# A streaming-encoder block on one core: the first feed-forward by Strassen pairs, its down products dealt out between them, and the modulation sums moved to ScalarE and GpSimd

## The chip, the core and the metric

One core of a Trainium2 chip runs the whole program. The metric is the time of one execution on the device in microseconds (us); a run's time is that of the execution, and the profile is of one execution taken by itself. The core has five engines with a queue each: TensorE (PE; its weight loads are counted apart as PEld), VectorE (DVE), ScalarE (ACT), GpSimd (POOL) and SyncE (SP), which here only issues DMAs. An engine works through its queue in order.

## The reference

One layer on x of 512 tokens by 1024 features, in float32:

```python
mod = silu(c) @ w_ada + b_ada                    # nine vectors of 1024: shift, scale, gate, three times
h = rms(x) * (1 + s1) + sh1
x = x + 0.5 * g1 * ((silu(gate) * up) @ w_out)   # gate, up = halves of h @ ffn1_w_in; 1024 -> 2 x 2816 -> 1024
h = rms(x) * (1 + s2) + sh2
x = x + g2 * mixer(h)                            # gated delta rule (4 heads) and latent attention (4 heads)
h = rms(x) * (1 + s3) + sh3
x = x + 0.5 * g3 * swiglu(h, ffn2_w_in, ffn2_w_out)
```

## The kernel before, in words

Activations lie feature-major: eight tiles `xT[t]` of 128 features by 512 tokens. Each float32 product is made of three matmuls (`mm3`, L265): both factors are split into a high part (a ScalarE cast, `hh`, `wh`, `ah`) and a low part (VectorE, value minus high part: `hl`, `wl`, `al`), and high x high, high x low and low x high are added up in PSUM.

Weights come as *units* of 128x1024 (`unit`, L204): an SP load into `wr`, a ScalarE cast to `wh`, a VectorE subtraction to `wl`; each of the three has four buffers. With `dma=True` the low part is made by a ScalarE copy with scale -1 and an adding DMA from GpSimd's queue. Everything of 128x512 floats in SBUF shares one pool of 56 *slots* (L86). A DMA into a slot stands in SP's queue until the slot is free.

The stages: **phase 0** (L297) normalises x and runs over the eight feature tiles `kt`. In each turn it makes one tile of the first two modulation vectors (the matmuls of L418, a ScalarE copy `sg` L421, the matmuls of L338 that read `sg`, then VectorE), modulates `h[kt+1]` (`modulate`, L450: VectorE, ScalarE `hh`, VectorE `hl`) and adds the products of `h[kt]` into six accumulators: the first three feed-forward tiles f=0..2, gate and up. **First feed-forward**: for f=3..21 two dense units each, 24 matmuls of 512 columns per unit (L656), and `glu` (L618), which makes `ah` and `al`. **Down** (L678): eight output tiles t, each of 22 products over f; the last two in token halves, so that the norm of the first half (`norm_half`, L483) runs under the second. **Mixer** (L1965): `latents`, then 16 dense units (k, q, v, z) with the attention and delta-rule work in between, then the output product. **Second feed-forward** (L736 on): the last 18 f by *Strassen pairs*: token halves, input halves and gate/up form a 2x2x2 block product, which is done with seven products of 12 matmuls of 256 columns (`product`, L856) in place of the eight that the dense form amounts to. The weights are summed on VectorE before (`sums`, `sums2`, L785 and L790) and split (`u`, `x`, `y`, `g1`); the token sums t1..t4 are made by `token_sums` (L742); the partial results are taken out of PSUM by `early_copy` (L812) before the next product adds to them. Steps s are numbered by hand: pair j takes the steps 7j+0, 1, 3, 4, 6, 9 and 12 (`STEPS`, L30), a planner (`add`, `tick`) puts the splits and copies at their steps, and `down` (L902) deals the down products out among the steps.

The other seven **modulation vectors** (14 chunks of 512 columns): `ada_rest` (L549) loads 128x512 tiles of `w_ada`, eight to a chunk, and adds scale x tile into an accumulator on VectorE (L575, L577); `ada_columns` (L590) sums four accumulators over the partitions on PE (L596), copies them (L599), transposes (L603) and adds the bias. It runs as a side task: eight chunks under the first feed-forward, six under the down products. `mixer_consts` (L1083: rope tables, small vectors) is a second side task of the first feed-forward.

Order: inside `in_order` (L133) each engine gets its instructions in the order in which the Python code makes them; inside `behind` they only stay behind the end of such a block; elsewhere the scheduler of the language picks the order. Before the change phase 0 and the second feed-forward are `in_order`; the first feed-forward after phase 0 is not.

## Time and profile before

| | |
|---|---|
| median of 3 runs | 1047.33 us (1045.64 to 1049.43) |
| profiled execution: span | 1044.0 us |
| phase 0 | about 0 to 64 us |
| first feed-forward and down | 64 to 404 us |
| mixer | 404 to about 690 us |
| second feed-forward | 690 to 1044 us |
| PE busy 690 to 732 us (entry of the second feed-forward) | 41.8 of 42 us |
| ACT / DVE busy 700 to 732 us | 16.9 / 26.4 of 32 us |
| DMA share, 20 to 60 us / 60 to 80 us | 1.04 (280 GB/s) / 0.91 (269 GB/s) |

The span goes from the first to the last instruction of the profiled execution; the device time is a few us longer. Matmuls overlap in the pipeline, so their price is the distance between the starts of neighbours and not the duration that a row shows. In a row of the timeline the columns are start, duration, engine, line, operation, output <- inputs, shape, and count when several are merged; in brackets the idle time before and what ended it. In a row of one line's instructions the numbers are shortest/median/longest duration in ns.

### The profile page before, as it was taken

Reading aid. Unit: us, or ns where it says so; the run is one execution under the profiler, and the core shown is the slowest. Engines: PE = TensorE matmul, PEld = TensorE weight load, DVE = VectorE, ACT = ScalarE, POOL = GpSimd, SP = SyncE. Lnnn points to the kernel's source line nnn. Section 1 sums busy time; section 2 is a strip of 40 time slices with the busy share of each in tenths; the row PEclk is TensorE's granted clock in tenths of the full one; section 3 lists DMA queues with packets and bytes.
Section 4 is the critical chain, followed back from the end, with each engine's and each line's share of the span. In section 5 each row is a group of like instructions: output and inputs, shape, how many; then the busy total and the mean of one; then the engine's idle time right before and its main releaser. Section 6 shows DMA issues by size and latency. Waiting matters only on the chain. (4 is left out here: it accounts for less than half of the span.)

```text
span 1044.0 us, 16057 instructions
## 1 busy us (share of the span) xinstructions
PE 1026.9 (98%) x6355; PEld 881.4 (84%) x6355; DVE 681.4 (65%) x1257; ACT 446.9 (43%) x778; POOL 46.8 (4%) x113
## 2 busy tenths in 40 slices
PE   7999999999999999999999999999999999999998
PEld 5788878788887799888878778898999999999986
DVE  4488884333486636648977656688778778777633
ACT  4343222232222226749567563465445444344422
POOL 1000000000000011100001111310000000000000
PEclk9999999999999999999999999999999999999999
DMA  9989963323586539711311211073423334323222
GB/s 274 292 245 316 305 205 101 95 87 96 185 280 227 159 98 240 180 41 40 101 42 36 72 42 41 22 162 101 142 81 102 109 95 121 93 90 111 72 61 81
DMA packets 203689, 136.88 MB, mean 131 GB/s; under 512 B 13777, under 2 KB 186590, under 8 KB 203614
## 3 DMA queue, kind: packets, MB, share of 16 engines
q1 hardware_dynamic: 202318, 131.14, 42.8%
q0 software_dynamic: 1296, 4.72, 2.4%
q8 instruction: 50, 0.82, 0.3%
q14 instruction: 25, 0.20, 0.1%
HBM read 128.63 MB, written 2.49 MB: 126 GB/s over the span
## 5 line engine op out<-in xcount | busy, mean ns | idle before, releaser
L267 PE MATMUL pa<-hh,wh 128*128 128x512 f32 (+1 forms) x565 | 216.4, 383 | 0.4 <-ACT hh L465 0.4
L193 ACT CAST wh<-wr 128x1024 fp32r<-128x1024 f32 (+1 forms) x106 | 107.9, 1019 | 251.6 <-PE pa L268 172.9
L268 PE MATMUL pa<-hl,wh 128*128 128x512 f32 (+1 forms) x565 | 214.8, 380 | 0.5 <-DVE hl L457 0.3
L269 PE MATMUL pa<-hh,wl 128*128 128x512 f32 (+1 forms) x565 | 214.4, 379 | 0.0
L198 DVE TENSOR_TENSOR wl<-wr,wh 128x1024 fp32r<-128x1024 f32 (+1 forms) x97 | 114.2, 1179 | 95.6 <-ACT wh L193 93.1
L267 PE MATMUL pa<-ah,wh 128*128 128x512 f32 (+1 forms) x396 | 145.6, 368 | 0.6 <-DVE xT L899 0.4
L268 PE MATMUL pa<-al,wh 128*128 128x512 f32 (+1 forms) x396 | 144.5, 365 | 0.0
L269 PE MATMUL pa<-ah,wl 128*128 128x512 f32 (+1 forms) x396 | 143.5, 362 | 0.0
L267 PEld LDWEIGHTS pa<-hh,wh 128*128 128x128 f32 x565 | 106.3, 188 | 24.3 <-issue 3.7
L269 PEld LDWEIGHTS pa<-hh,wl 128*128 128x128 f32 x565 | 106.3, 188 | 21.0 <-issue 1.2
L268 PEld LDWEIGHTS pa<-hl,wh 128*128 128x128 f32 x565 | 106.4, 188 | 19.4 <-DVE hl L457 0.9
L269 PEld LDWEIGHTS pa<-ah,wl 128*128 128x128 f32 x396 | 74.8, 189 | 12.0
L267 PEld LDWEIGHTS pa<-ah,wh 128*128 128x128 f32 x396 | 75.2, 190 | 10.4 <-ACT wh L193 1.7
L268 PEld LDWEIGHTS pa<-al,wh 128*128 128x128 f32 x396 | 75.2, 190 | 7.2
L577 DVE SCALAR_TENSOR_TENSOR aa<-ar,sc,aa 128x512 f32<-128x512 f32 x98 | 73.0, 748 | 8.0 <-DMA ar<-in_w_ada 6.8
L872 PE MATMUL pb<-fh,wh 128*128 128x256 f32 x144 | 40.7, 283 | 0.0
L874 PE MATMUL pb<-fh,wl 128*128 128x256 f32 x144 | 40.7, 283 | 0.0
L874 PE MATMUL pb<-hh,wl 128*128 128x256 f32 x144 | 40.7, 283 | 0.0
L873 PE MATMUL pb<-fl,wh 128*128 128x256 f32 x144 | 40.7, 283 | 0.0
L873 PE MATMUL pb<-hl,wh 128*128 128x256 f32 x144 | 40.7, 282 | 0.0
L899 DVE SCALAR_TENSOR_TENSOR xT<-pa,mod,xT 128x512 f32<-128x512 f32 (+1 forms) x40 | 29.3, 735 | 17.3 <-PE pa L269 17.3
L872 PE MATMUL pb<-hh,wh 128*128 128x256 f32 x144 | 40.6, 282 | 0.0
(439 smaller groups left out, 1995.1 us busy)
## 6 DMA issues: line engine op xcount, KB each, us to landing
wr<-in_ffn_w_in SPq DMA_DIRECT2D x82, 512.0 KB, 3.9
ar<-in_w_ada SPq DMA_DIRECT2D x48, 512.0 KB, 6.0
wr<-in_ffn_w_out SPq DMA_DIRECT2D x34, 512.0 KB, 3.4
ar<-in_w_ada SPq DMA_DIRECT2D x48, 256.0 KB, 4.8
wr<-in_w_in SPq DMA_DIRECT2D x21, 512.0 KB, 3.7
wr<-in_ffn_w_out SPq DMA_DIRECT2D x17, 384.0 KB, 3.3
wl<-wr POOLq DMA_DIRECT2D x9, 512.0 KB, 6.2
wr<-in_w_out SPq DMA_DIRECT2D x8, 512.0 KB
```

The lines of the kernel that those rows point to most:

```text
L193: self.nc.scalar.copy(hi, raw)
L198: self.nc.vector.tensor_tensor(out=lo, in0=raw, in1=hi.bitcast(F32), op=ALU.subtract)
L267: mm(out, wh, xh, start=start, stop=False)
L268: mm(out, wh, xl, start=False, stop=False)
L269: mm(out, wl, xh, start=False, stop=stop)
L577: nc.vector.scalar_tensor_tensor(out=acc, in0=a, scalar=sc, in1=acc, op0=ALU.mult, op1=ALU.add)
L872: mm(out, wh, xh, start=start and k == 0, stop=False, **kw)
L873: mm(out, wh, xl, start=False, stop=False, **kw)
L874: mm(out, wl, xh, start=False, stop=stop and k == 3, **kw)
L899: nc.vector.scalar_tensor_tensor(out=self.xT[t][:, ts], in0=p[:, ts], scalar=gate[:, t:t + 1], in1=self.xT[t][:, ts], op0=ALU.mult, op1=AL ...
```

## The change

The first feed-forward now uses the same code as the second: f=0..2 come from phase 0, f=3 and 4 from four dense units (6..9), and f=5..21 are 17 Strassen pairs. The function `ffn2_rest` becomes `ffn_pairs`, with an entry (`enter1`, `enter2`) and an end (`leave1`, `leave2`) for each feed-forward. The token sums of the first feed-forward are made in phase 0, two calls a turn in the turns kt=3..6. The down products over f=0..15 are dealt out between the steps from s=9 on, those over f=16..21 stand at the end, tiles 4..7 in token halves. Everything from phase 0 to there is one `in_order` block. The modulation sums leave VectorE: ScalarE scales a tile (in place, but for the first of a chunk) and GpSimd adds it to the accumulator. Chunks 0..5 run in the entry (13 calls of two tiles) and in the first steps (two calls a step); chunks 6..13 and most of `mixer_consts` run as a fourth side task of the mixer's dense units.

```diff
@@ phase0
-        t, m = self.slot(s="hm"), self.slot(s="hm")
+        t, m = self.slot(s="hm"), self.tm[0]
...
-                    self.modulate([kt + 1], slice(0, NT), rb, self.c2, self.c1)
+                    self.modulate([kt + 1], slice(0, NT), rb, self.c2, self.c1, self.tm)
                     if kt == 0:
                         w = weights(kt + 1)
+                if j == 4 and kt >= KT // 2 - 1 and more:
+                    for which in range(2):
+                        drain(self.token_sums(kt + 1 - KT // 2, which))
+                if j == 1 and not more:
+                    tail()
@@ ada_rest becomes ada
+    def ada(self, chunks):
...
+        steps = [(c, kc) for c in chunks for kc in range(KT)]
...
+        for i in range(3):
+            load(i)
+        for i, (c, kc) in enumerate(steps):
+            a, sc = tiles.pop(i), self.sc[:, kc:kc + 1]
+            if kc == 0:
+                acc = self.slot(s="aa")
                 accs.append(acc)
+            out = acc if kc == 0 else a
+            nc.scalar.activation(out, a, AF.Copy, scale=sc)
+            if kc:
+                nc.gpsimd.tensor_tensor(out=acc, in0=acc, in1=a, op=ALU.add)
+            load(i + 3)
+            if i % 2:
+                yield
+        yield
+        yield from self.ada_columns(chunks[0], accs)
@@ ffn1
+        def tail():
+            for i in range(6, 10):
+                raws[i] = self.raw_unit(w1, i)
+            for i in (6, 7):
+                drain(self.unit_split(raws, split, i))
+        with self.in_order():
+            with self.tc.tile_pool(name="p0", bufs=3) as self.p0:
+                pu = self.phase0(tail)
+            accs = {i: pu[i // 2 + 3 * (i % 2)] for i in range(6)}
+            with self.tc.tile_pool(name="ws", bufs=1) as self.ws:
+                side, self.consts = Side(), self.mixer_consts()
+                side.add(self.ada((0, 1, 2, 3)), self.ada((4, 5)))
+                leave = self.ffn_pairs(w1, ins["ffn1_w_out"][0], lambda: self.mod[2], FIRST, raws, split, accs, self.enter1, side)
+        with self.tc.tile_pool(name="wx", bufs=2) as wx:
+            with self.behind():
+                nb = leave(wx)
@@ enter1 (products(i): one dense unit on PE; unit, of, glu: one half now, the VectorE half after the next entry's first half)
+        step = (side.step,)
+        side.step()
+        self.staggered([glu(0), step, (products, 6), unit(8), (do["load"],), glu(1), step, unit(9), (products, 7), step, glu(2),
+                        step, (do1["load"],), step, (products, 8), glu(3), step, of(do["sums"]), step, of(do["sums2"]), step,
+                        of(do["u"]), step, (products, 9), step, of(do["x"]), step, of(do["y"]), step, glu(4), of(do["g1"])])
@@ ffn_pairs
-        d0 = down(0, 4, 1, 1.3)
-        for c in (1, 2):
-            down(4 * c, 4, 28 * c + 10, 32 / 28)
-        down(12, 4, 94, 1.28)
+        if side:
+            d0, r = None, 128 / 103
+            for c in range(4):
+                down(4 * c, 4, stop - 103 + c * 32 / r, r)
...
             if s in last:
                 steps_of(*last[s])
+            if side:
+                side.step(2)
+                if s in (stop, stop + 8):
+                    next(self.consts)
...
+        def leave1(pool):
+            for t in (6, 7):
+                unit_hi(t, pool)
+                unit_lo(t)
+            halves = [slice(0, HALF), slice(HALF, NT)]
+            with self.matmuls_in_order(self.ends[mybir.EngineType.PE]):
+                for half, ts in enumerate(halves):
+                    for t in range(4, KT):
+                        for k in (0, 3):
+                            steps_of(t, k, k + 3, ts)
+                            if half and (t, k) in ((5, 0), (6, 3), (7, 3)):
+                                next(na, None)
+                        finish(t, ts, ends[t])
+                        self.square_in(t, ts, accum)
+                        if half and t in (4, 6):
+                            self.prefetch(t // 2 - 1)
+                    if half == 0:
+                        self.new_h()
+                        na = self.norm_half(0, accum, 3)
+                drain(na)
+                self.prefetch(3)
+            return self.norm_half(1, accum, 3)
@@ mixer
+        ada.add(self.consts, self.ada((6, 7)), self.ada((8, 9, 10, 11)), self.ada((12, 13)))
-        self.dense_units(4, Rates(sides, (1, 0, 0.25)), 1, conv_done(4, kT))
+        self.dense_units(4, Rates(sides, (1, 0, 0.25, 1)), 1, conv_done(4, kT))
-        self.dense_units(4, Rates(sides, (0.75, 0, 1.5)), 1, conv_done(0, qT))
+        self.dense_units(4, Rates(sides, (0.75, 0, 1.5, 1)), 1, conv_done(0, qT))
-        self.dense_units(4, Rates(sides, (0.75, 0.5, 1)), 1, conv_done(8, vT))
+        self.dense_units(4, Rates(sides, (0.75, 0.5, 1, 0.5)), 1, conv_done(8, vT))
-        self.dense_units(4, Rates(sides, (1, 0.75, 2)), 1, z_done)
+        self.dense_units(4, Rates(sides, (1, 0.75, 2, 0.5)), 1, z_done)
+        ada.flush()
```

More of the change, by code (lines that the diff above doesn't have):

```diff
@@ L333, in phase0 @@
         self.new_h()
+        self.new_sums(self.c1)
+        self.tm = [self.slot(s="tm") for _ in range(KT)]
         def columns(kt, sg, pg):
@@ L994, in ffn2_rest @@
-        for g in steps:
-            if isinstance(g, tuple):
-                g[0](*g[1:])
-                continue
-            next(g, None)
-            if waiting:
-                next(waiting, None)
-            waiting = g
-        next(waiting, None)
+        enter(raws, split, products, lambda f: self.glu_steps(accs, f), pairs, d0, side, w1)
         k0, m = 16, 6
@@ L1020, in steps_of @@
         def steps_of(t, a, b, ts=full):
-            if a == 0 and t not in ends:
-                ends[t] = self.aux() if t == 3 else self.acc()
+            if t not in ends:
+                ends[t] = self.aux() if t in ((3, 6, 7) if side else (3,)) else self.acc()
             self.dense(ends[t], units[t][1:], self.act[k0:], ts, a, b, m - 1)
@@ new lines, in leave2 @@
+        def leave2(pool):
+            for t in range(4, KT - 1):
+                steps_of(t, 0, m)
+                for e in range(2 * t - 8, min(2 * t - 6, t)):
+                    self.store(e, range(NB))
+                if t + 2 < KT:
+                    unit_hi(t + 2)
+                    unit_lo(t + 2)
+                finish(t, full, ends[t])
+            t = KT - 1
+            ends[t] = self.acc()
+            for half in range(2):
+                ts = slice(half * HALF, half * HALF + HALF)
+                steps_of(t, 0, m, ts)
+                finish(t, ts, ends[t])
+                if half == 0:
+                    self.store(t - 1, range(NB))
+                else:
+                    self.store(t, range(2))
+            self.store(t, range(2, 4))
@@ L1079, in bc @@
+        return leave1 if side else leave2
     def bc(self, col, n, w=P):
```

311 lines of the change are left out of this document (107 added, 204 removed).

## The prediction

> **What bounds the kernel now.** I read the page's head first, then the chain that ended last, then stretches.
>
> ```profile
> span 1044.0 us, 16057 instructions
> PE 1026.9 (98%) x6355; PEld 881.4 (84%) x6355; DVE 681.4 (65%) x1257; ACT 446.9 (43%) x778; POOL 46.8 (4%) x113
> ...
> PEclk9999999999999999999999999999999999999999
> ...
> PE 38%; DVE 1%; issue 1%; ACT 1%; POOL 0%; POOLq 0%; DVEq 0%
> ```
>
> PE is never without work for long, and at full clock; what the chain shows of other engines is 3%. The stretches view (length, then busy us and count of PE, PEld, DVE, ACT, POOL) says the same stage by stage:
>
> ```profile
> 64.10:404.00 339.90, 339.90 (x1652) 282.94 (x1650) 206.26 (x327) 101.55 (x132) 8.52 (x16) 1.00 0.60 182
> 440.00:600.00 160.00, 159.41 (x981) 128.31 (x979) 116.10 (x322) 100.83 (x208) 11.81 (x24) 1.00 0.22 57
> ```
>
> From 64 to 404 us, the stage that is rewritten, PE has no gap at all. So fewer matmuls are worth their full price, and any wait put into PE's queue costs its full length.
>
> **The matmuls: minus 13.5 us.** The price is the distance between starts (start, duration, engine, line, operands).
>
> ```profile
> 66.13 0.39 PE L267 MATMUL pa<-hh,wh 128*128 128x512 f32 x1
> 71.57 0.39 PE L267 MATMUL pa<-hh,wh 128*128 128x512 f32 x1
> 851.13 0.28 PE L872 MATMUL pb<-hh,yh 128*128 128x256 f32 x1
> 852.56 0.40 PE L267 MATMUL pa<-ah,wh 128*128 128x512 f32 x1
> 853.25 0.28 PE L872 MATMUL pb<-fh,wh 128*128 128x256 f32 x1
> L267 PE MATMUL pa<-ah,wh 128*128 128x512 f32 x132 | 51.7, 392 | 0.0
> L267 PE MATMUL pa<-ah,wh 128*128 128x256 f32 x88 | 25.3, 287 | 0.0
> ```
>
> A dense unit of 24 matmuls takes 71.57 - 66.13 = 5.44 us, 0.227 each. A Strassen product (12 of 256 columns) takes 852.56 - 851.13 = 1.43 us, 0.119 each, and three down matmuls between two products 0.69 to 0.70 us, 0.233 each. A pair's f costs 48 x 0.227 = 10.89 us dense and 84 x 0.119 = 10.0 by pairs; times 17, -15.2 us. Down was (the two rows of groups, times three) 396 x 0.227 + 264 x 0.119 = 121.2 us; it becomes 128 x 3 x 0.233 + 72 x 0.227 + 144 x 0.119 = 122.9, +1.7. Sum -13.5 us. The same code in the second feed-forward runs without gaps, so the steps from about s=9 on should too.
>
> **Phase 0: plus 9 us.** The token sums go into queues that are in order. One turn, and the prices of the sums from the second feed-forward:
>
> ```profile
> 47.61 0.75 DVE L457 SCALAR_TENSOR_TENSOR hl<-hm,sh,hh 128x512 fp32r<-128x512 f32 x1 [0.79 <-ACT hh L465]
> 48.40 1.09 PE L418 MATMUL pb<-ar,sc 128*32 128x256 f32 x16
> 49.58 0.37 ACT L421 COPY sg<-pb 128x256 f32<-128x256 f32 x1 [2.00 <-PE pb L418]
> 50.91 0.50 PE L338 MATMUL pb<-sel,sg 128*128 128x1 f32 x4
> 54.18 1.09 PE L418 MATMUL pb<-ar,sc 128*32 128x256 f32 x16
> L752 DVE TENSOR_TENSOR tv<-tm x4: 418/419/420, 700.2 to 707.9; 128x256 f32<-128x256 f32 x4
> L753 DVE SCALAR_TENSOR_TENSOR tv<-tm,mod,tv x4: 480/484/487, 700.9 to 708.3; 128x256 f32<-128x256 f32 x4
> L763 ACT CAST fh<-tv x8: 620/622/628, 701.5 to 725.5; 128x512 fp32r<-128x512 f32 x8
> L765 DVE TENSOR_TENSOR fl<-tv,fh x8: 682/685/693, 702.2 to 726.5; 128x512 fp32r<-128x512 f32 x8
> ```
>
> A turn is 54.18 - 48.40 = 5.78 us and VectorE ends it with `hl` at 48.36. Now two sums follow, each drained at once: 0.1 + 0.42 + 0.48 on VectorE, the cast 0.62, `fl` 0.69, 2 x 0.48, the second cast 0.62, less the overlap of neighbours: 3.8 us until ScalarE is free. Behind that cast stands `sg` of the next turn: 52.1 to 52.5, not 49.58. PE's L338 is due at 50.91 and waits 1.5 us. That turn's split, `hh` and `hl` are late as well, so the later turns start the sums 0.8 us after PE's turn begins and each L338 waits 2.4 us. Sums after kt=3, 4, 5 delay the L338 of three turns: 1.5 + 2.4 + 2.4. After kt=6 no L338 is left, but `hl` of the last tile is 0.65 us late, and the first dense unit's low part, behind two sums, one cast (0.95) and one subtraction (1.22), comes 6.85 us into the last turn where PE asks at about 4.9: 2.0. Sum 8.9, I take 9. Below it: 0, if the order in the block were not what the code says; above: 12, if DMA, 0.9 to 1.0 busy here, is late too.
>
> **The entry: plus 28 us.** The prices:
>
> ```profile
> 439.89 2.56 ACT L1308 ACTIVATE uh<-ur,cwT 128x512 fp32r<-128x512 f32 x4
> 59.04 1.99 ACT L193 CAST wh<-wr 128x1024 fp32r<-128x1024 f32 x2
> L621 ACT ACTIVATE sg<-pa x22: 584/587/592, 60.9 to 270.4; 128x512 f32<-128x512 f32 x22
> L623 DVE TENSOR_TENSOR af<-sg,pa x19: 676/687/690, 75.5 to 275.3; 128x512 f32<-128x512 f32 x19
> L626 DVE TENSOR_TENSOR al<-af,ah x22: 680/684/693, 65.7 to 277.3; 128x512 fp32r<-128x512 f32 x22
> L198 DVE TENSOR_TENSOR wl<-wr,wh x97: 951/1224/1227, 25.7 to 657.3; 128x1024 fp32r<-128x1024 f32 x81, 128x768 fp32r<-128x768 f32 x16
> L1232 POOL TENSOR_TENSOR Sg<-S,gl x2: 1040/1040/1041, 631.6 to 643.1; 128x512 f32<-128x512 f32 x2
> 377.43 1.23 DVE L198 TENSOR_TENSOR wl<-wr,wh 128x1024 fp32r<-128x1024 f32 x1 [0.52 <-ACT wh L193]
> 377.80 1.45 POOL L481 TENSOR_TENSOR na<-na,sq 128x256 f32<-128x256 f32 x1 [101.46 <-ACT sq L479]
> 665.10 0.74 POOL L481 TENSOR_TENSOR na<-na,sq 128x256 f32<-128x256 f32 x1
> ar<-in_w_ada SPq DMA_DIRECT2D x48, 256.0 KB, 4.8
> ```
>
> I count from the start of phase 0's last turn. *PE*: the unit held above ends at 12.1, three more at 28.4, and two products with a short wait for `u`'s low part at 31.8. There, in step s=2, stands `ada_columns` of chunks 0..3: 13 calls in the entry and two a step make the 18th call, the one that issues it, fall in s=2. Being in order, PE can do nothing else until the 32nd tile is added up.
>
> *ScalarE* starts on the side task at 6.45. Until the 32nd tile it has 32 scalings x 0.615 (four of the same form in 2.46 us between starts) = 19.7; five glus, in each of which it waits for VectorE between `sg` and `ah`, x 1.85 = 9.3; six casts of 128x1024 x 0.95 = 5.7; 0.8 more. It is through at 42.0, and GpSimd at 43.1: PE waits 11.3 us. The columns then cost 0.8 more than before, as transposes stand right behind their copy. The second group (chunks 4, 5) stands in s=7. ScalarE must first take a partial result out of PSUM after s=3 (47.8), then 12 scalings, one cast of each size: 57.0, GpSimd 58; PE is there at 52.1: 5.9. Together 18 us from ScalarE alone. SP's queue adds no reserve: 48 of these tiles (last row: 256 KB each) and the first pairs' weights are some 16 MB in 60 us, about 270 GB/s; and a tile's load that waits for a slot, which only GpSimd's add sets free, holds the pairs' weight loads behind it.
>
> *GpSimd* makes it longer. A 128x512 operation took it 1.04 us, and the 128x256 add of 665.10 took 0.74, but 1.45 when it began under VectorE's `wl<-wr,wh`: that ended at 378.66, 0.86 us into the add. Two operands in SBUF on VectorE seem to hold GpSimd up. If they exclude each other, the first group ends no earlier than 7.7 + 28 adds x 1.04 + VectorE's two-operand work (five `al`, five low parts of 1.22, one of 0.69, six sums of 0.68: 14.3) = 51.1, and PE waits 19.3; the second 14 x 1.04 + 7.1 later, 72.8, where PE is at 60.0: 12.8. Together 32 us. With adds at 0.74 the port is no bound and 18 stays; with 1.46, twice the 128x256, it is 50. I take 28: near the port's sum with the one row of the full width, as some of VectorE's work falls into time when GpSimd has nothing to add.
>
> The Trainium skill ("SBUF — State Buffer", section "SBUF: two separate sides") speaks against this change here: GpSimd and a VectorE instruction with two SBUF inputs take one port pair by an exclusive lock, held for a whole instruction. The trace agrees at 377.80, where 0.74 became 1.45. Its "GPSIMD Engine Reference", section 3.1, gives 4497 ns for a GpSimd add of 2048 columns; a quarter of it, 1.12 us, is an estimate from that page, and with it the port's sum would be 3 us longer.
>
> **The end of down: plus 5 us.** The second half of tiles 4..7 (24 x 0.357 = 8.6 us) must cover the first half's norm, where 44 x 0.357 = 15.7 us did.
>
> ```profile
> 384.35 0.48 DVE L685 SCALAR_TENSOR_TENSOR xT<-pa,mod,xT 128x256 f32<-128x256 f32 x1 [5.69 <-PE pa L269]
> 390.35 0.59 PE L445 MATMUL pb<-dg,ones 128*128 128x256 f32 x2
> 400.85 0.28 PE L267 MATMUL pa<-hh,wh 128*128 128x256 f32 x1
> 402.73 0.49 DVE L457 SCALAR_TENSOR_TENSOR hl<-hm,mod,hh 128x256 fp32r<-128x256 f32 x1 [0.18 <-ACT hh L465]
> ```
>
> Now the last `hl` of that half comes 18.9 us after the first half's last `finish`, just as PE reaches it. After, PE reaches it at about 9.6 + 2.5 = 12; the norm can be there at 14.5 at best (spread at 7.5, then eight tiles of 0.8 on VectorE), at 18.9 if nothing gets faster. 2 to 7, I take 5: the splits for the mixer's first units stand in the same stretch.
>
> **The mixer: plus 4 us.** 64 scalings x 0.615 = 39 us are added to ScalarE's 100.8 of 160 us (the row above), 56 adds to GpSimd's 11.8, the rope tables to VectorE's 116. All still fit, PE's 159.4 of 160 has no slack, and waits there are scheduled, not forced: 0 to 10. Less than 0 is excluded, as PE has no gap there, nor in down, that work taken from VectorE could close.
>
> **Sum.** -13.5 + 9 + 28 + 5 + 4 = +32.5 us on the profiled execution, whose span is 1044.0; the median of the runs is 1047.33, 3.3 us of it outside the span, which nothing here changes. 1047.3 + 32.5 = **1080 us**. The case's own range takes the entry from 24 to 50, the end from 2 to 7, the mixer from 0 to 10: +21.5 to +62.5, 1069 to 1110.
>
> **The rivals.**
> *Order by readiness (faster).* If the engines' queues in the block did not bind as the code reads, with `sg` and the casts issued ahead of the sums and scalings, phase 0 and the entry would cost nothing. It decides at `sg`: it must start within 1.3 us of L418's end in turns 4 to 6. Then -13.5 + 2 to 9: 1036 to 1043, say 1037. For it: the second feed-forward's entry, with the same eight token sums, ran without a gap. Against: that entry has five units on PE over it and no scalings.
> *The entry fits, phase 0 doesn't.* If the adds and scalings reach PE's two places in time, but for 5 us, the sum is -13.5 + 9 + 5 + 2 to 5 = about +3, 1050; no change. It needs 0.30 us a scaling in place of 0.615.
> *No shared port.* 18 in the entry: +22, 1070.
> *The pairs save nothing.* They would have to cost 0.130 us a matmul; the row says 0.119, so it gets no chance of its own.
>
> **How the numbers follow.** Forecast 0.5, of it 0.05 beyond 1100; no shared port 0.2; entry fits 0.1; order by readiness 0.2. A run of three can tell 0.3%, 3.1 us, from no change. Faster by more than that: 0.2; within: 0.09; slower: 0.71. Leaving out the fastest part of the one rival and what lies above 1100, the range is 1038 to 1100.
>
> **What would show it.** Steps: a dense unit and a product at the same 5.44 and 1.43 us; in phase 0 an idle PE before L338, three times, ended by `sg`; in the entry PE idle before the `ada_columns` matmuls, twice, ended by GpSimd's adds, over 10 us the first time; GpSimd's adds longer than 1.04 us where VectorE subtracts; a gap before the mixer's first products ended by `hl`. It is wrong if PE stays at 98%, or if the adds take under 0.8 us.

## The result, and the profile after

The changed kernel takes 1157.73 us (1156.54 to 1162.03, four runs) against 1046.92 us (1045.64 to 1049.43, four runs) of the kernel before on the same chip: 1.106 times as long, with a 95% interval of 1.104 to 1.109. The forecast was 1080 us, from 1038 to 1100. The sign was right, and the size was out by more than the whole growth that was forecast: 111 us came where 33 were expected.

The head of the page of the changed kernel, and the shares of its chain that ended last:

```profile
span 1154.8 us, 17725 instructions
...
PE 1054.9 (91%) x6911; PEld 916.5 (79%) x6911; DVE 770.9 (67%) x1362; ACT 562.9 (49%) x999; POOL 189.0 (16%) x213
...
PEclk9997679999999998999999969999999999999999
...
PE 71%; DVE 10%; ACT 7%; POOL 5%; issue 4%; DMA 2%; SPq 0%; POOLq 0%; ACTq 0%; DVEq 0%
```

PE has fallen from 98% to 91%. The chain now leaves PE for VectorE, ScalarE, GpSimd, the issue of instructions and DMA, for 28% of the span; before, they had some 3%, in a chain whose shares add up to only 41%. And PE's granted clock falls in three places, most in the fourth to sixth of the 40 slices (87 to 173 us) and in the 24th (664 to 693).

The first and the last start of the dense half units that stand at the mixer's and at the second feed-forward's head cut the span into three (the view of one source line: durations min/median/max, first and last start). First the kernel before, then the changed one:

```profile
L510 PE MATMUL pa<-hh,wh x32: 280/283/468, 404.1 to 695.6; 128*128 128x256 f32 x32
```

```profile
L522 PE MATMUL pa<-hh,wh x32: 278/283/561, 460.0 to 806.4; 128*128 128x256 f32 x32
```

To the mixer 404.1 became 460.0 (+55.9). The mixer, 291.5, became 346.4 (+54.9). What follows took 1044.0 - 695.6 = 348.4 and takes 1154.8 - 806.4 = 348.4. So half of the loss lies where the forecast looked for all but 4 us of it, and half in a stage that it had down for 4.

**The entry.** The start of phase 0's last turn and PE's longer waits behind it in the changed kernel's timeline (start, duration, instruction, and in brackets the idle time before it with what ended it), then GpSimd's adds, and then the stretches view (length; PE, PEld, DVE, ACT, POOL busy and count; clock; DMA share; GB/s):

```profile
68.09 0.39 PE L271 MATMUL pa<-hh,wh 128*128 128x512 f32 x1
...
101.23 0.58 PE L865 MATMUL pb<-hh,wl 128*128 128x256 f32 x1 [4.96 <-DVE wl L800]
111.85 1.91 PE L599 MATMUL pb<-aa,ones 128*32 128x512 f32 x2 [4.83 <-POOL aa L586]
122.55 1.92 PE L599 MATMUL pb<-aa,ones 128*32 128x512 f32 x2 [8.79 <-POOL aa L586]
135.82 0.58 PE L863 MATMUL pb<-fh,yh 128*128 128x256 f32 x1 [5.16 <-ACT uc L807]
145.43 1.92 PE L599 MATMUL pb<-aa,ones 128*32 128x512 f32 x2 [4.77 <-POOL aa L586]
155.69 1.92 PE L599 MATMUL pb<-aa,ones 128*32 128x512 f32 x2 [8.35 <-POOL aa L586]
```

```profile
80.88 41.61 POOL L586 TENSOR_TENSOR aa<-aa,ar 128x512 f32<-128x512 f32 x25 [1.37 <-ACT ar L584]
134.17 21.47 POOL L586 TENSOR_TENSOR aa<-aa,ar 128x512 f32<-128x512 f32 x14 [11.67 <-ACT ar L584]
```

```profile
100.00:120.00 20.00, 7.70 (x28) 4.92 (x28) 13.66 (x10) 10.18 (x16) 19.14 (x13) 0.59 0.37 114
120.00:140.00 20.00, 11.51 (x50) 9.57 (x51) 4.54 (x6) 7.24 (x11) 8.02 (x6) 0.59 0.48 171
140.00:160.00 20.00, 6.88 (x21) 3.28 (x20) 7.09 (x6) 7.69 (x14) 14.93 (x11) 0.58 0.38 118
160.00:180.00 20.00, 20.00 (x140) 18.47 (x139) 15.28 (x23) 8.08 (x12) 0.00 (x0) 0.99 0.27 79
```

The mechanism of the forecast is there to the letter: PE stands in front of `ada_columns` (L599), twice for each group, until GpSimd's adds end. The first group ends at 122.5, 54.4 us after phase 0's last turn began at 68.1 (the first row above, of which the turn has six), where 51.1 were worked out. But ahead of those waits (at 101.23) and between them (at 135.82) there are others, of 5 us each, for a split that VectorE and a copy that ScalarE made late. PE is busy 26 of the 60 us from 100 to 160, at a clock of 0.59. From 160 on PE runs without a gap.

**The mixer.** The whole stage in the stretches view, before and after, and the longest wait of the changed kernel's PE in it (timeline):

```profile
404.00:695.50 291.50, 286.30 (x2069) 240.49 (x2069) 199.40 (x516) 172.64 (x360) 35.21 (x56) 1.00 0.31 81
```

```profile
460.00:806.00 346.00, 309.45 (x2094) 250.95 (x2095) 236.73 (x579) 211.61 (x423) 110.33 (x143) 0.94 0.37 106
```

```profile
673.83 1.08 PE L1952 MATMUL pb<-ident,on 128*128 128x128 f32 x4 [8.05 <-DVE on L1228]
```

PE's idle time grew from 5 to 37 us, and its busy time by 23 us at a lower clock. No other engine is near its limit over the stage: VectorE has 237 of 346 us, ScalarE 212, GpSimd 110. No single wait is longer than the 8 us shown. The profile alone doesn't say which part of the moved work this is; the experiments below take it apart.

### The profile page after: what moved, and what is told of

Its sections match the earlier page's. It is cut to its first block, busy times and chain, and to the rows that moved or that the text cites. A ratio compares the mean times of both kernels' runs of the same rounds, so it can differ in the third digit from the quotient of the medians.

```text
span 1154.8 us, 17725 instructions
## 1 busy us (share of the span) xinstructions
PE 1054.9 (91%) x6911; PEld 916.5 (79%) x6911; DVE 770.9 (67%) x1362; ACT 562.9 (49%) x999; POOL 189.0 (16%) x213
## 4 chain that ended last, share of the span: by engine, by line
PE 71%; DVE 10%; ACT 7%; POOL 5%; issue 4%; DMA 2%; SPq 0%; POOLq 0%; ACTq 0%; DVEq 0%
PE pa L271 11%; PE pa L272 10%; PE pa L273 10%; PE pb L863 10%; PE pb L864 9%; PE pb L865 9%; POOL aa L586 5%; DMA ar<-in_w_ada 2%; ACT ar L584 1%; DVE wl L207 1%; DVE cv L1434 1%; PE pb L273 1%; PE pb L271 1%; PE pb L272 1%; ACT hh L477 1%
## 5 line engine op out<-in xcount | busy, mean ns | idle before, releaser
L586 POOL TENSOR_TENSOR aa<-aa,ar 128x512 f32<-128x512 f32 x98 | 139.6, 1426 | 185.5 <-ACT ar L584 141.7
L271 PE MATMUL pa<-hh,wh 128*128 128x512 f32 (+1 forms) x277 | 105.4, 380 | 5.4 <-ACT hh L477 2.1
L272 PE MATMUL pa<-hl,wh 128*128 128x512 f32 (+1 forms) x277 | 103.9, 375 | 1.4 <-DVE hl L469 0.9
L273 PE MATMUL pa<-hh,wl 128*128 128x512 f32 (+1 forms) x277 | 103.4, 373 | 0.5 <-DVE wl L207 0.5
L865 PE MATMUL pb<-hh,wl 128*128 128x256 f32 x280 | 80.8, 289 | 5.0 <-DVE wl L800 5.0
L863 PE MATMUL pb<-hh,wh 128*128 128x256 f32 x280 | 80.8, 289 | 0.8 <-ACT wh L795 0.8
L864 PE MATMUL pb<-hl,wh 128*128 128x256 f32 x280 | 80.6, 288 | 0.0
L584 ACT ACTIVATE ar<-ar,sc 128x512 f32<-128x512 f32 x98 | 66.7, 719 | 11.4 <-DMA ar<-in_w_ada 10.0
L271 PEld LDWEIGHTS pa<-hh,wh 128*128 128x128 f32 x277 | 53.1, 192 | 19.0 <-issue 4.2
L273 PEld LDWEIGHTS pa<-hh,wl 128*128 128x128 f32 x277 | 52.9, 191 | 10.9 <-DVE wl L207 1.4
```

The source lines that it names most:

```text
L271: mm(out, wh, xh, start=start, stop=False)
L272: mm(out, wh, xl, start=False, stop=False)
L273: mm(out, wl, xh, start=False, stop=stop)
L584: nc.scalar.activation(out, a, AF.Copy, scale=sc)
L586: nc.gpsimd.tensor_tensor(out=acc, in0=acc, in1=a, op=ALU.add)
L863: mm(out, wh, xh, start=start and k == 0, stop=False, **kw)
```

## The experiments

Each run is one execution, with its profile. Two readings are used throughout: the start of the mixer ("to mixer") and its length, taken from the same source line as above. What follows the mixer is within 1 us of 348.4 in every run that is read below by its stages. For scale: single runs of the kernel before, made beside them, took 1046.03 to 1049.17.

| run | to mixer | mixer | time, us |
|---|---|---|---|
| before | 404.1 | 291.5 | 1046.92 |
| changed | 460.0 | 346.4 | 1157.73 |
| no_adds | 432.6 | 332.6 | 1114.96 |
| mixer_no_adds | 459.7 | 332.5 | 1141.97 |
| vector_sums | 442.9 | 339.7 | 1132.37 |
| mixer_vector_sums | 459.3 | 339.3 | 1148.40 |
| mixer_loads_only | 459.5 | 318.8 | 1128.11 |
| mixer_no_rope | 461.3 | 322.1 | 1133.13 |
| mixer_no_sums | 459.2 | 294.6 | 1103.60 |
| mixer_neither | 460.9 | 295.5 | 1106.11 |
| no_entry_mixer_columns | 407.1 | 302.7 | 1059.85 |
| entry_loads_mixer_loads | 425.7 | 311.1 | 1086.82 |
| order_in_phase0 | 455.8 | 348.0 | 1153.75 |
| before_scalar_gpsimd | 416.4 | 291.8 | 1058.28 |
| no_sums | 405.0 | 293.9 | 1048.65 |
| no_sums_sums_order | 404.6 | 314.0 | 1068.38 |
| sums_no_columns_held | 405.0 | 342.1 | 1096.89 |
| mixer_loads_held | 404.9 | 311.6 | 1066.29 |
| mixer_loads_own | 404.8 | 307.4 | 1061.98 |
| after_own | 462.5 | 344.7 | 1157.01 |

### GpSimd's adds

Everywhere (no_adds), or in the mixer alone (mixer_no_adds, with `c > 5`):

```diff
-            if kc:
-                nc.gpsimd.tensor_tensor(out=acc, in0=acc, in1=a, op=ALU.add)
```

> The changed kernel without GpSimd's 98 adds of the modulation sums (each acc keeps only its first row block's product, so the seven other row blocks are left out of the sums); ScalarE's scalings, the loads and the columns stay where they are, and the static order of the tensor engine moves in about one row of a hundred. Theory A, the adds delay the columns and hold VectorE's port: the mixer loses 40 to 55 of its 55 us of growth and the entry 20 to 34 of its 52, so 1068 to 1098 us. Rival B, ScalarE's scalings and the loads set the columns: within 10 of the changed kernel's 1158. Rival C, the entry is the adds' but the mixer's 55 us come from something else that moved (the rope tables, the order): the entry loses 20 to 34 and the mixer nothing, 1124 to 1138.

> As the run without adds, but only for chunks 6 to 13, those summed in the mixer; the entry keeps its adds. Theory A: the mixer, 346 us from its first matmul to the first of the second feed-forward, falls to 291 to 306, the time to 1103 to 1118. Rivals B and C: the mixer stays within 8 us of 346 and the time at 1150 to 1160. The stretch ahead of the mixer stays at 460 by all of them.

The entry loses 27.4 us, as theories A and C had it; the mixer loses 13.9, which is neither A's 40 to 55 nor C's nothing. The total, 1115, falls between their ranges. So leaving out the adds takes away half of the entry's loss and a quarter of the mixer's. The two stages don't disturb each other: the mixer is 332.6 and 332.5 us with a different entry. That allowed later runs to make one edit in each stage.

How the adds act on VectorE is seen at a very small instruction of the mixer (one source line; min/median/max ns). First the changed kernel, then the run without adds:

```profile
L1930 DVE SCALAR_TENSOR_TENSOR va<-al x8: 160/164/1267, 613.2 to 709.9; 128x2 f32<-128x2 f32 x8
```

```profile
L1928 DVE SCALAR_TENSOR_TENSOR va<-al x8: 141/161/165, 577.4 to 668.3; 128x2 f32<-128x2 f32 x8
```

Two columns a partition take 0.16 us, but beside the adds as much as 1.27, about the length of one add. In the changed kernel's timeline three of the eight are long (1.06, 1.27 and 1.09 us, from 613.23, 617.04 and 645.64), and these three lie within runs of adds; the five of 0.16 lie outside them. The forecast had GpSimd stand behind VectorE; it also goes the other way. That is the exclusive lock, held for a whole instruction, of the Trainium skill's "SBUF — State Buffer", section "SBUF: two separate sides", and the row agrees with it in size.

### The sums on VectorE, in the places of the change

vector_sums, and for the mixer alone mixer_vector_sums:

```diff
-            nc.scalar.activation(out, a, AF.Copy, scale=sc)
-            if kc:
-                nc.gpsimd.tensor_tensor(out=acc, in0=acc, in1=a, op=ALU.add)
+            if kc:
+                nc.vector.scalar_tensor_tensor(out=acc, in0=a, scalar=sc, in1=acc, op0=ALU.mult, op1=ALU.add)
+            else:
+                nc.vector.tensor_scalar(out=acc, in0=a, scalar1=sc, scalar2=None, op0=ALU.mult)
```

> The changed kernel with all 112 steps of the modulation sums as one VectorE instruction each, in the same places, nothing of them on ScalarE or GpSimd; the result is the reference's. Theory A: VectorE's 0.75 us a step lie where it has room in the entry only in part; the entry loses 15 to 30 us and the mixer 30 to 50, 1080 to 1110. Rival B (ScalarE's queue and the loads): if the queue, the same as A; if the loads, the entry loses less than 8. Rival C: mixer stays, 1125 to 1143.

> The same for chunks 6 to 13 alone. Theory A: the mixer falls by 30 to 50 of its 55 us, 1108 to 1128. Rival C: within 8 of 1158. If VectorE is itself the mixer's bound (it is at 20.00 of 20 us busy in one stretch of the changed kernel), the time rises by up to 64 times 0.75 = 48 us.

With 1132.37 us the first lands in C's range; the second gains 7.1 us in the mixer, less than A asked and more than C. One VectorE instruction a step, which the kernel before used, is 25 us better here than the pair of ScalarE and GpSimd, though VectorE is the busier engine. But 85 us of the 111 stay: the larger part isn't the choice of engine.

### The mixer taken apart

Four kernels without the mixer's sums in some part. mixer_loads_only reads the last loaded tile of each chunk as if it were the sum; mixer_no_sums replaces the three `ada` generators by constants; mixer_no_rope leaves out the mixer's adds and sets the rope tables to a constant, mixer_neither leaves out sums and tables. The edit of mixer_no_sums:

```diff
-        ada.add(self.consts, self.ada((6, 7)), self.ada((8, 9, 10, 11)), self.ada((12, 13)))
+        ada.add(self.consts)
+        for j in (5, 6, 7, 8):
+            self.mod[j] = self.const([P, 8], s="mod")
+            nc.gpsimd.memset(self.mod[j], 0.1)
```

> Chunks 6 to 13 are loaded, and each column is made from the last row block's tile as it was loaded: the 64 scalings on ScalarE and the 56 adds on GpSimd are left out, loads and columns stay. The run without the mixer's adds had a mixer of 332.5 us, 41 above the 291.5 of the kernel before. Theory S, ScalarE's 64 scalings (45 us in its queue, 172 us to 217) push the casts and copies of attention back: the mixer falls by 25 to 41 us, to 291 to 307 and the time to 1100 to 1117. Theory R, the rope tables and norm columns that now come at the mixer's start are what is late: it stays within 5 us of 332 and the time at 1137 to 1147. Theory D, the loads of the sums hold up the weights and the copies through DRAM: the same, no gain.

> As the run without the mixer's adds, and the rope tables (positions, angles, sines, cosines, some 70 small VectorE instructions, 14 us) are constants set by GpSimd instead of computed in the mixer. Theory R: the mixer falls by 20 us or more, to 312 or less, the time to 1122 or less. Theory S: at most 8 us of 332, the time 1134 to 1142. Theory D: nothing.

> Chunks 6 to 13 are left out altogether (loads, scalings, adds, columns; their vectors are constants), the rope tables stay in the mixer. Theory S: 5 us (the columns) to 8 below the run with loads alone. Theory D: 25 to 41 us below the run without the mixer's adds, while the run with loads alone gains nothing. Theory R: within 10 of 1142.

> Neither the sums of chunks 6 to 13 nor the rope tables are computed (constants in their place): the mixer holds then less than that of the kernel before, which computed no sums but had the tables ready too. If sums and tables are the whole of it, the mixer is 288 to 294 us and the time 1098 to 1104. Rival O, the static order or what the mixer finds when it starts (weights not yet there, a late ScalarE) costs of itself: the mixer stays 10 us or more above 291.5.

Without the scalings the mixer falls by a further 13.7 us, about half of the least that theory S asked for. Without loads and columns it falls by 24.2 more, where S had 5 to 8, to 294.6, and is then 3.1 us above the kernel before. The rope tables cost nothing when no sums are there (294.6 and 295.5) and 10.4 beside loads and scalings (332.5 and 322.1): not a cost of their own, then, but one that comes up only beside the sums. So theory R falls in the form that it had (10.4 lies between its 20 and S's 8), S explains a quarter, and with the sums out neither what the mixer finds at its start nor the order that it then has costs more than 4 us (rival O asked for 10).

### Loads against columns, and the entry

One edit in each stage:

```diff
# no_entry_mixer_columns: no sums in the entry; in the mixer columns of constant tiles
+                    if i == 0:
+                        accs.append(self.slot(s="aa"))
+                        nc.gpsimd.memset(accs[-1], 0.1)
# entry_loads_mixer_loads: loads alone; columns only for c < 6
-            nc.scalar.activation(out, a, AF.Copy, scale=sc)
-            if kc:
-                nc.gpsimd.tensor_tensor(out=acc, in0=acc, in1=a, op=ALU.add)
+            if kc == 7:
+                accs[-1] = a
...
-        yield from self.ada_columns(chunks[0], accs)
+        if chunks[0] < 6:
+            yield from self.ada_columns(chunks[0], accs)
```

> Two edits in two stages. Chunks 0 to 5 are left out (no loads, scalings, adds or columns; their vectors are constants), and in the mixer the columns of chunks 6 to 13 are made from tiles that GpSimd sets to a constant: no loads, scalings or adds there. Start to mixer: if the sums are the whole of the entry's growth, 404 - 13.5 (matmuls) + 9 (token sums of phase 0) + 7 (end of the down products) = 406, between 402 and 412; if another part of the change costs there, above 420. Mixer (294.6 without sums, 318.8 with loads and columns): theory D, the 64 loads take slots and the queue, 297 to 303; theory C, the tensor engine stands in order behind the columns, 310 to 319. Time 1053 to 1063 by D, 1066 to 1080 by C.

> Two edits in two stages. Chunks 0 to 5: loads and columns stay, the columns are made from the last row block's tile as loaded (no scalings, no adds). Chunks 6 to 13: the 64 loads stay, nothing reads them and there are no columns; the vectors are constants. Start to mixer (460 with all, 432.6 without adds): if the 48 loads at 300 to 390 GB/s hold the entry, 420 to 432; if ScalarE's scalings do, 408 to 416. Mixer: theory D 310 to 319, theory C 295 to 302.

In the mixer both count: columns 302.7 - 294.6 = 8.1, loads 311.1 - 294.6 = 16.5, and 24.6 together is what mixer_loads_only had shown (24.2). Both mixers lie in theory D's ranges, at the upper and the lower end: the loads are two thirds, but C's columns are the last third. The columns are PE's own work rather than a wait: in the first of these mixers PE is busy 296.5 us and idle 6.2, in no_sums 288.0 and 5.9.

Without the entry's sums the mixer starts at 407.1 here, and at 405.0 in a later run (no_sums): inside the 402 to 412 expected. Loads and columns bring it to 425.7, inside the range given for loads that hold the entry. In entry_loads_mixer_loads a row of PE's waits there (us in all, times, longest) and two stretches say how:

```profile
PE pb L597 <- DMA ar<-in_w_ada: 10.8, 3, 4.4
```

```profile
64.00:100.00 36.00, 34.13 (x156) 27.25 (x154) 25.01 (x38) 16.10 (x24) 0.00 (x0) 0.96 0.91 302
100.00:120.00 20.00, 11.85 (x56) 8.21 (x56) 8.01 (x11) 5.44 (x9) 0.00 (x0) 0.70 0.80 278
```

The transfers run at 302 GB/s with the DMA engines 91% busy, and PE waits for them 10.8 us in front of the columns, which read one tile of each chunk as it was loaded; nothing is scaled or added. Then the scalings add 6.9 us (425.7 to 432.6) and the adds 27.4.

### Two orders, and one part of the change alone

order_in_phase0 puts the token sums behind the next turn's column products and weight casts, and four squares behind two casts at the end of the down products:

```diff
-                if j == 4 and kt >= KT // 2 - 1 and more:
-                    for which in range(2):
-                        drain(self.token_sums(kt + 1 - KT // 2, which))
+                if j == 0 and kt >= KT // 2:
+                    drain(*(self.token_sums(kt - KT // 2, which) for which in range(2)))
```

> The changed kernel with two reorderings, the whole of the reference computed: each pair of token sums in phase 0 comes behind the next row's column products and weight casts, its two halves interleaved, and the squares of the first four outputs at the end of the down products come behind the casts of the last two weight units. By the forecast's working the waits of phase 0's column sums (1.5 + 2.4 + 2.4 us, and up to 2.6 of its tail) and the 2.4 us behind the squares go: start to mixer 460 to between 450 and 454, the time 1147 to 1152. Rival: the token sums only wait elsewhere, 0 to 3 us, 1155 to 1158.

It gains 4.2 us ahead of the mixer, less than the 6 to 10 forecast and more than the rival's 0 to 3. The waits of the changed kernel's column sums, which are the forecast's to a few tenths (1.5, 2.4, 2.4),

```profile
46.78 0.60 PE L344 MATMUL pb<-sel,sg 128*128 128x1 f32 x4 [1.30 <-ACT sg L433]
54.99 0.61 PE L344 MATMUL pb<-sel,sg 128*128 128x1 f32 x4 [2.13 <-ACT sg L433]
63.20 0.61 PE L344 MATMUL pb<-sel,sg 128*128 128x1 f32 x4 [2.15 <-ACT sg L433]
```

are gone, 5.6 us, and so are the 2.4 behind the squares. In their place PE waits for `hh` of the next tile, 2.9 us in the rows below, and for its `hl`, 0.9, which leaves the 4.2:

```profile
50.84 0.50 PE L271 MATMUL pa<-hh,wh 128*128 128x512 f32 x1 [1.19 <-ACT hh L476]
57.59 0.50 PE L271 MATMUL pa<-hh,wh 128*128 128x512 f32 x1 [0.35 <-ACT hh L476]
64.35 0.49 PE L271 MATMUL pa<-hh,wh 128*128 128x512 f32 x1 [1.38 <-ACT hh L476]
```

before_scalar_gpsimd is the kernel before with its sums as ScalarE scalings and GpSimd adds:

```diff
-                        if kc + e == 0:
-                            nc.vector.tensor_scalar(out=acc, in0=a, scalar1=sc, scalar2=None, op0=ALU.mult)
-                        else:
-                            nc.vector.scalar_tensor_tensor(out=acc, in0=a, scalar=sc, in1=acc, op0=ALU.mult, op1=ALU.add)
+                        nc.scalar.activation(a if kc + e else acc, a, AF.Copy, scale=sc)
+                        if kc + e:
+                            nc.gpsimd.tensor_tensor(out=acc, in0=acc, in1=a, op=ALU.add)
```

> The kernel before with one part of the change alone: its modulation sums, where they are, as 112 scalings on ScalarE and 98 adds on GpSimd in place of 112 VectorE instructions. They lie spread over the first feed-forward and the down products there. Theory of place (the cost lies in where the sums come, not in the engines): within 8 us of 1047. Rival, the adds cost wherever they are (27 us in the entry and 14 in the mixer of the changed kernel): 1062 to 1090.

1058.28 against 1046.20 of the kernel before beside it: 12 us, between the two ranges. All of it lies ahead of the mixer (416.4), and nearly all in one stretch, the first of these two (length, then busy us):

```profile
120.00:160.00 40.00, 32.97 (x131) 25.82 (x132) 25.67 (x34) 21.30 (x31) 24.74 (x17) 0.87 0.76 226
280.00:320.00 40.00, 40.00 (x178) 33.16 (x177) 18.01 (x16) 22.89 (x32) 25.40 (x25) 1.00 0.72 236
```

Both stretches have some 25 us of GpSimd, and the second costs nothing. PE's two longest waits ahead of the mixer from 60 us on, 3.8 us each, are both for VectorE (`af` and `rw`). Spread out, the pair of engines is cheaper than in the entry but not free; that place decides the rest is what the two stretches suggest, not what a run shows.

### No sums at all; the order, the work, the places

Two parts of the mixer's loss, loads and scalings, are waited for by hardly any instruction of PE. But with them the planner puts PE's instructions in another order: 749 of the 1613 that the program has there stand elsewhere, dense units earlier and attention later. Three kernels hold PE to a given order (edit below, with a list of places): one without sums to the order with them, two with sums to the order without. They stand against one without any sums:

```diff
-    nb = k.mixer(nb)
+    with k.traced() as block:
+        nb = k.mixer(nb)
+    held = [i for i in block if i.engine == mybir.EngineType.PE]
+    for a, b in zip(PE_ORDER, PE_ORDER[1:]):
+        k.follow(held[b], held[a].name)
```

> The changed kernel with no modulation sums at all (all 14 chunks left out, their vectors constants): the pairs and the moved tables alone. From the stages measured: 407 to the mixer, 295 in it, 348 behind it and 2 around the span, 1050 to 1054. If the stages do not add up, outside that.

> No sums at all, but the tensor engine's instructions of the mixer are held in the order that they have when the mixer's sums are there (loads, scalings and adds, without columns); 749 of the 1613 stand elsewhere by that. Theory O (the order carries the cost of loads and scalings): the mixer takes 310 to 330 us and the time 1066 to 1086. Theory W (the work itself carries it): the mixer stays at 293 to 299 us, the time 1050 to 1056.

> No sums in the entry; in the mixer the loads, scalings and adds of chunks 6 to 13 without their columns (vectors constants), with the tensor engine's instructions of the mixer held in the order of the kernel without sums. In its own order this mixer would take 346 - 8 = 338 us. Theory O: with the order held only the adds' 14 us are left, 302 to 314 us, 1058 to 1072. Theory W: 330 to 345 us, 1086 to 1102.

> No sums in the entry; in the mixer the 64 loads alone, nothing reads them, with the tensor engine's instructions held in the order of the kernel without sums. In its own order this mixer took 311.1 us. Theory O: 294 to 299 us, the time 1050 to 1056. Theory W (slots and queue): 308 to 314 us, 1064 to 1070.

no_sums came 1.4 us under its range, at 1048.65. The order without the work costs 20 us (314.0), as theory O had it. The work without the order costs as much as with it: 311.6 against 311.1 for the loads, and 342.1 against some 338 (an estimate, 346 less the columns' 8) for all but the columns, as theory W had it. Each is enough by itself and they don't add up. So the other order isn't needed to make the work dear; the work costs as much in either order.

Last, the loads into three tiles of their own, by themselves and in the full changed kernel:

```diff
-                tiles[i] = self.slot(s="ar")
+                tiles[i] = self.ad.tile([P, NT], F32, tag="ar", name=self.name("ar"))
...
-        self.late_enter(12)
+        self.late_enter(9)
```

> No sums in the entry; in the mixer the 64 loads alone, nothing reads them, no columns, as in the run whose mixer took 311.1 us, but into three tiles of their own and not into the pool of 56 that the mixer's other tiles come from (the pool for late tiles has 9 places for that, not 12). Queue, number and bytes are the same. Theory P (places in the shared pool): the mixer is back at 293 to 299 us, the time 1048 to 1054. Theory Q (the queue, or the bytes): it stays at 308 to 314 us, 1063 to 1069.

> The changed kernel whole, with the mixer's 64 loaded tiles in three places of their own; the accumulators stay in the shared pool. Start to mixer stays at 460. Theory P: the loads' 16.5 us go in large part, the mixer 328 to 336 us and the time 1139 to 1148. Theory Q: within 3 us of 346 and 1158.

307.4 us lies between the ranges, 0.6 below Q's, and the full kernel, with 1.7 gained in the mixer and 0.7 in all, lies in Q's: theory P falls as the main cause. Where a large part of the loads' cost now lies is seen in mixer_loads_own (waits of ScalarE and PE in the mixer, then a stretch at its start):

```profile
ACT wh L202 <- DMA wr<-in_w_in: 14.8, 1, 14.8
...
PE pa L271 <- ACT uh L1306: 5.9, 1, 5.9
```

```profile
427.00:447.00 20.00, 14.01 (x64) 11.06 (x63) 5.42 (x9) 4.67 (x8) 1.04 (x1) 0.88 0.88 257
```

As nothing reads these tiles, they are all fetched in the first 90 us of the mixer (issued up to 492.1), and there ScalarE waits 14.8 us for a weight that stands behind 17 of them in SP's queue. That shows one way in which the loads cost time, the queue or the bytes that they share with the weights. That it is the same in the changed kernel, where the loads are spread over 180 us, isn't shown: another queue for them wasn't tried. By what mechanism the loads cost 16.5 us there stays open.

## Why the prediction was wrong, step by step

Every step of the sum beside what the runs give for it:

| step | forecast | measured | from |
|---|---|---|---|
| matmuls, phase 0, end of down | -13.5 + 9 + 5 = +0.5 | +0.9 | no_sums 405.0, before 404.1 |
| entry | +28 (24 to 50) | +55.0 | changed 460.0, no_sums 405.0 |
| mixer | +4 (0 to 10) | +54.9 | 346.4 and 291.5 |
| second feed-forward | 0 | 0.0 | 348.4 and 348.4 |

**The first line came out right in part by luck.** Phase 0's term was right: its three waits are within 0.3 us of their working, and the first dense unit starts 8.1 us later than before (72.15 in no_sums, 64.09 before). But no_sums makes no column sums on PE, and these took about 6 us of the 404.1 before (an estimate from the gaps that four groups of them make between their neighbours' starts, 1.1 and 0.4 us each). And the end of the down products cost about 12 us, not 5. Three rows of PE in no_sums, the first half-tile matmul, the first on the normed half, and the mixer's first dense unit:

```profile
372.57 0.36 PE L271 MATMUL pa<-ah,wh 128*128 128x256 f32 x1 [0.41 <-DVE xT L909]
395.91 0.28 PE L271 MATMUL pa<-hh,wh 128*128 128x256 f32 x1
405.02 0.56 PE L522 MATMUL pa<-hh,wh 128*128 128x256 f32 x1
```

The first distance is 23.3 us, where 144 x 0.119 = 17.1 were worked out; the second is 9.1, where the kernel before had 3.3 (400.85 to 404.1). The changed kernel takes the same 32.4 us there (427.57 to 460.0). So two errors of some 6 us cancel, and with them the line reads -13.5 + 8.1 + 12 - 6 = +0.6. It also says something that the forecast had in hand and didn't dwell on: the matmuls saved are paid back by what prepares and follows them. With no modulation sums at all the changed kernel takes 1048.65 us where the kernel before, which makes them, takes 1046.69. With phase 0 and the end of down as they are there was nothing to win, however the sums are placed; order_in_phase0 shows that some 4 us of these two can be had back.

**The entry was mis-sized.** The step was: "Together 18 us from ScalarE alone", with the shared port 32, and "I take 28". The wait that it priced was of that size: PE stands 13.6 and 13.1 us in front of the two groups' columns (the L599 rows above), 26.7 in all. The entry's other 28 us are what the step didn't count. Taken out one after the other, the parts cost: adds 27.4, scalings 6.9, loads with columns 18.6 to 20.7 (from 407.1 or 405.0 to 425.7). The prices were partly off: an add took not the 1.04 us of the row used, which is of another operation, but 1.26 at the least and 1.54 in the mean, and the second group ended 87.6 us after the turn's start where 72.8 were worked out. A scaling kept its price, 0.62 us from start to start (72.89 and 73.51); the 714 below is a duration. Rows of the changed kernel, from 60 to 160 us:

```profile
L586 POOL TENSOR_TENSOR aa<-aa,ar 128x512 f32<-128x512 f32 x42 | 64.4, 1537 | 77.9 <-ACT ar L584 75.3
...
L584 ACT ACTIVATE ar<-ar,sc 128x512 f32<-128x512 f32 x42 | 28.1, 714 | 6.4 <-DMA ar<-in_w_ada 6.2
L584 ACT ACTIVATE aa<-ar,sc 128x512 f32<-128x512 f32 x6 | 4.3, 722 | 14.0 <-DMA ar<-in_w_ada 14.0
```

What was missing is the loads. The forecast wrote that "SP's queue adds no reserve" and worked out 270 GB/s, and then gave it no microseconds; the last row shows ScalarE standing 14.0 us for the first tile of the second group (whether for the bytes, for SP's queue or for a slot that an add had to free isn't separated). A resource that is said to be full is a term of the sum. Missing too was what PE does after a wait (below). The rivals fared no better: "no shared port" is excluded by the row of `va<-al` and by adds of up to 2.24 us where 1.26 is the shortest, "the entry fits" by 55 us, "order by readiness" by the waits for `sg` and L599 above.

**The mixer is the step that failed.** It read: "All still fit, PE's 159.4 of 160 has no slack, and waits there are scheduled, not forced: 0 to 10." It summed busy time by engine, found room on each, and so priced 64 scalings, 56 adds and the rope tables at 4 us; the 64 loads and the columns of eight chunks stand in no term of it. The runs give, from 346.4 us down: adds 13.9, scalings 13.7, loads with columns 24.2, of which columns alone are 8.1 and loads alone 16.5. Room on an engine's average wasn't the bound. The sentence itself says that PE has no slack there, which was the reason to expect the opposite.

Why, as far as the profile can be read: the mixer is a set of chains through PE, ScalarE and VectorE that just kept PE fed; what makes a link late, a queue ahead of a cast, a port held for 1.3 us, shows in PE at the chains' end, where no dense unit is left to cover it. For that speak attention's transposes (L1952, a wait of 8 us behind the last dense unit) and the 10% of VectorE in the chain of the whole run. It is a reading and not shown by a run of its own, and for the loads and the scalings the link that they delay was not found.

## What to carry to other kernels

Where one engine is 98% busy over a stage, work added to the others isn't free because their sums fit; price it by leaving parts out (loads, scalings, adds, columns), one at a time. Parts taken out one after the other add up by construction; the one check of it here is that loads and columns, each alone, give 24.6 us where both together give 24.2. The rope tables, the work and the order are a warning: they do not add up. Take the gain alone first, with the side work left out altogether: that one run would have shown that these pairs, as they stand here, save nothing. And a transfer that is moved to where the DMA engines are full (91% busy here) is a term of its own, even if the engines that use it are idle.

## What the runs showed of the hardware that had not been expected

A wait costs PE more than its length. After the wait that ends at 101.23 the changed kernel's timeline goes on like this (start, duration):

```profile
101.61 0.41 PE L863 MATMUL pb<-hh,wh 128*128 128x256 f32 x1
101.83 0.41 PE L864 MATMUL pb<-hl,wh 128*128 128x256 f32 x1
102.04 0.41 PE L865 MATMUL pb<-hh,wl 128*128 128x256 f32 x1
...
105.45 0.35 PE L863 MATMUL pb<-hh,wh 128*128 128x256 f32 x1
105.64 0.28 PE L864 MATMUL pb<-hl,wh 128*128 128x256 f32 x1
105.76 0.28 PE L865 MATMUL pb<-hh,wl 128*128 128x256 f32 x1
```

From 101.23 to 105.45, 4.2 us, the matmuls start 0.213 us apart (the second 0.38 behind the first), then 0.12: the 19 of that time would have taken 2.3 us, so the wait of 4.96 us costs 1.9 more. Not every wait does this: after those of 1.30 and 2.13 us at 46.78 and 54.99 (above) matmuls of 512 columns go on 0.23 apart. In the entry such waits follow each other closely, and the stretches there have a granted clock of 0.58 to 0.59. The Trainium skill's "TensorE: Matmul & The Clock Gate", Part 1 on the clock gate, has the array at half clock after idling, until about 3.4 us of steady work have passed; the 0.213 and the 4.2 us here agree with it in kind. The forecast counted every wait at its bare length.

The same happens in the mixer, and it is where most of the loads' cost is paid. The mixers of no_sums and of entry_loads_mixer_loads, where the 64 loads are all that is added, and a stretch of the second (length; PE, PEld, DVE, ACT, POOL busy and count; clock; DMA share; GB/s):

```profile
405.00:698.90 293.90, 287.95 (x2070) 242.26 (x2070) 211.35 (x571) 172.00 (x360) 35.49 (x87) 0.99 0.27 68
425.70:736.80 311.10, 298.93 (x2070) 249.38 (x2071) 213.03 (x571) 172.44 (x360) 35.49 (x87) 0.96 0.41 118
646.00:666.00 20.00, 20.00 (x198) 14.66 (x197) 7.99 (x16) 10.01 (x21) 0.00 (x0) 0.54 0.01 2
```

The loads add 6.2 us of waits to PE and 11.0 us of busy time for the same 2070 matmuls. In the 20 us from 646 PE is busy throughout at a clock of 0.54, which alone is 9 us of work at full clock not done (an estimate, 0.46 of 20); ahead of it, from 606 to 646, PE has 8 us of gaps, none longer than 2.4.
